# Expert stage of a two-layer backbone: two or five weight units converted late and none on GpSimd, plain group order in layer two, and in layer one each slot's row of g2 gathered from a table

## The chip, the cores and the metric

The kernel runs on one core of a Trainium2 chip. The metric is the device time of one execution in microseconds; the time shown is a median of runs, and one further execution was recorded by the profiler.

## The reference

Two layers run over a stream of 256 context tokens and 1024 latent tokens of width 1024. Each layer mixes tokens and then sends every token to two of 16 experts (top group of four, top two experts inside it). What matters here is the expert part:

```python
def expert_block(args):
    xblk, e = args
    return (jax.nn.silu(xblk @ w1[e]) * (xblk @ w3[e])) @ w2[e]
...
out = jnp.zeros((n_tok + 1, d), h.dtype).at[slot_tok].add(yb * slot_w[:, None])
...
        if last:
            x = x + g2 * hier_moe(h2, *moe_args).reshape(bsz, n_lat, d)
        else:
            ...
            f = hier_moe(jnp.concatenate([h2c, h2], axis=0), *moe_args)
            ctx = ctx + cg2 * f[:bsz * n_ctx].reshape(bsz, n_ctx, d)
            x = x + g2 * f[bsz * n_ctx:].reshape(bsz, n_lat, d)
```

So a token's expert output is scaled by its routing weight and by a row of 1024 gains. In layer one (`last` false) that row is `g2` for latent tokens and `cg2` for context tokens; in layer two only latent tokens are left and there is one row.

## The kernel before

**Blocks.** A router sorts tokens into slots by expert. An expert's slots are worked off in blocks of 128 rows; the expert stage walks the 16 experts in the order of the list `eo`, and for each of them runs first what goes beyond 128 slots (under `tc.If(cnt > P)`): a full second block (`block(x1, ...)`) if there are more than 192, and a half block of 64 rows (`block_half`) for what is left over or for 129 to 192 slots. Then comes the base block, `block(x0, ...)`, which every expert has. An expert with a base block alone is called small here. A block is two passes over the weight units 0 to 3 and 4 to 7 (w1 and w3, into `hps`), a product `g` (ScalarE L1654, VectorE L1655), its transpose on TensorE (L1637, `gtp`), and a pass over units 8 to 11 (w2, into `yps`).

**Weight units.** Each expert has 12 units of 128x1024 fp32 (512 KB). SyncE fetches them into eight buffers `eraw`. A unit is converted before use: ScalarE writes the rounded high part (L1578), then VectorE, or GpSimd for units 5 and 11, writes the rest (L1580). `mm3` multiplies high by high, high by low and low by high. Conversions of the next expert's units stand inside the base block of the expert before: `side(u)` is called after each step u = 0 to 11 and converts one unit or two. A converted unit goes to one of 13 buffers `ew`, so at most one unit more than an expert's own twelve fits.

**Slots.** `gather` (GpSimd indirect DMA, L1590) brings the token rows of a block from `h2s`; for the base and second block of the expert after next it is issued in `side`, for the third block at L1876. `prep` turns them around on TensorE (L1608, `xtp`) and splits them (L63, L64, L1611) inside the base block before. `scatter` multiplies by gain and weight (VectorE L1626 in layer one, L1624 in layer two) and adds the rows into `xb` by an indirect DMA (L1627).

**Gains.** In layer one the gain rows are built per block in `gain`: ScalarE scales one row (L1618), VectorE adds the other (L1619), with a weight that is zero for the tokens of the other kind. In layer two the row is the same for all slots.

**Order.** The engines work off their queues in the written order (`tc.manual_schedule()`). GpSimd's queue holds, for each base block: the scatter of the block before, the third block's gather, unit 5, two gathers, then the scatter, then unit 11. The indirect DMAs use eight semaphores in turn. Where a branch is skipped, GpSimd executes instructions (`ISA` in the listings) that bring these semaphores to the counts of the other path, and these wait until the transfers that still hold one have landed.

**What runs.** By the trace, the blocks of the 16 positions of `eo` are (F a second block, h a half block, B the base block): layer one, order of groups 0, 2, 1, 3: B, FhB, B, FhB, B, FhB, B, hB, B, FB, hB, FhB, B, FhB, B, B. Layer two, the same order of groups: FB, hB, B, B, FhB, hB, B, B, hB, hB, B, B, FhB, hB, B, B. There groups 1 and 3 hold the small experts.

## Time and profile before

| what | us |
|---|---|
| median of 3 runs | 2846.44 (2843.09 to 2849.04) |
| the profiled execution | 2843.8 |
| its span, first to last instruction | 2842.0 |
| mean granted TensorE clock in it | 0.946 of full speed |

The page of that execution gives PE 2531.7 us busy (89% of the span), DVE 1827.6 (64%), ACT 1244.5 (44%) and POOL 775.1 (27%). A share says little by itself: the program has stages with different limits. The two expert stages are the stretches from 932.3 to 1493.6 us and from 2277.5 to 2809.9 us of the span. A timeline row reads: start, length, engine, line, operation, output and input by the program's names, count, and in brackets how long the engine had been idle and what ended that. A row of the view by stretches has its length, then busy time and count of PE, PEld, DVE, ACT and POOL, the granted clock, the busy share of the DMA engines and GB/s.

### The profile page before, as it was taken

The page shows a single profiled execution, that of the slowest core. Times are in us where ns is not written, and L with a number is a line of the kernel's source. Part 1 is how long each engine was busy: PE and PEld are TensorE (multiplying, and loading weights), DVE is VectorE, ACT ScalarE, POOL GpSimd, SP SyncE. Part 2 cuts the span into 40 slices and gives each one's busy share as a digit, 9 for nine tenths or more (in the row PEclk, how much of TensorE's full clock was granted, in tenths as well). Part 3 has the DMA queues.
Part 4 walks back from the last instruction along what each step waited for, and adds up shares of the span by engine and source line. Part 5 has one row for each costly group of instructions (what it writes and reads, how often), then busy time and mean ns, then how long its engine had stood idle before and what let it go on. Part 6 is the DMA issues. An engine that isn't in the chain of part 4 may idle for free. (4 is left out here: it accounts for less than half of the span.)

```text
span 2842.0 us, 41623 instructions
## 1 busy us (share of the span) xinstructions
PE 2531.7 (89%) x15412; PEld 2127.4 (75%) x15412; DVE 1827.6 (64%) x3173; ACT 1244.5 (44%) x2060; POOL 775.1 (27%) x514
## 2 busy tenths in 40 slices
PE   6999998898898899899997999979989788989894
PEld 3878887788686677677776898868977666767673
DVE  3314665777478777776775317748866858587776
ACT  3313213566323555555554322127652346465453
POOL 0000113401144344344430001123023425354442
PEclk8999999999999899999998999999999889999997
DMA  8374217431224777787775352264223468596856
GB/s 297 114 241 140 83 69 204 86 73 31 98 112 158 251 249 250 242 274 225 242 236 185 99 173 79 75 163 87 66 63 110 171 238 306 186 322 211 312 187 245
DMA packets 159551, 493.68 MB, mean 174 GB/s; under 512 B 18896, under 2 KB 40016, under 8 KB 158768
## 3 DMA queue, kind: packets, MB, share of 16 engines
q1 hardware_dynamic: 110336, 361.14, 38.1%
q0 software_dynamic: 29312, 99.39, 12.0%
q10 hardware_dynamic: 19552, 28.84, 2.8%
q8 instruction: 176, 2.88, 0.4%
q14 instruction: 175, 1.43, 0.2%
HBM read 408.75 MB, written 79.15 MB: 172 GB/s over the span
## 5 line engine op out<-in xcount | busy, mean ns | idle before, releaser
L1580 DVE TENSOR_TENSOR ew<-eraw,ew 128x1024 fp32r<-128x1024 f32 x318 | 466.3, 1489 | 40.2 <-ACT ew L1578 35.3
L1578 ACT ACTIVATE ew<-eraw 128x1024 fp32r<-128x1024 f32 x384 | 390.9, 1054 | 73.7 <-DMA eraw<-in_experts_dram 61.2
L212 PE MATMUL ps<-hh,w 128*128 128x256 f32 x2096 | 289.4, 292 | 17.7 <-PEq L751 5.1
L1627 POOL DMA_INDIRECT xb<-yt,yx x54 | 182.1, 3372 | 431.6 <-DVE yt L1626 259.6
L212 PEld LDWEIGHTS ps<-hh,w 128*128 128x128 f32 x2096 | 269.2, 197 | 27.4 <-ACT hh L319 5.7
L67 PE MATMUL hps<-ew,x 128*128 128x512 f32 x656 | 275.8, 420 | 7.3 <-PEq L1831 3.6
L69 PE MATMUL hps<-ew,x 128*128 128x512 f32 x656 | 264.7, 403 | 3.2 <-DVE x L64 3.2
L962 DVE TENSOR_REDUCE mx<-S 128x1 f32<-128x1280 f32 (+1 forms) x144 | 196.9, 1370 | 107.9 <-PE S L957 106.4
L68 PE MATMUL hps<-ew,x 128*128 128x512 f32 x656 | 265.4, 405 | 0.0
L970 ACT ACTIVATE pe<-S,mx 128x1280 f32<-128x1280 f32 (+1 forms) x144 | 177.4, 1232 | 47.6 <-DVE mx L962 40.1
L1580 POOL TENSOR_TENSOR ew<-eraw,ew 128x1024 fp32r<-128x1024 f32 x66 | 178.4, 2703 | 17.2 <-ACT ew L1578 9.1
L956 PE MATMUL S<-kk,qh 128*128 128x512 f32 (+1 forms) x400 | 158.3, 396 | 17.5 <-ACT pe L970 8.6
L67 PEld LDWEIGHTS hps<-ew,x 128*128 128x128 f32 x656 | 129.4, 197 | 40.5 <-issue 9.5
L69 PEld LDWEIGHTS hps<-ew,x 128*128 128x128 f32 x656 | 128.3, 196 | 34.0 <-DVE x L64 3.6
L212 PE MATMUL ps<-hl,w 128*128 128x256 f32 x1048 | 149.4, 286 | 0.0
L68 PEld LDWEIGHTS hps<-ew,x 128*128 128x128 f32 x656 | 129.5, 197 | 25.6
L67 PE MATMUL ps<-wv,hh 128*128 128x256 f32 (+1 forms) x480 | 142.2, 296 | 0.0
L957 PE MATMUL S<-kk,ql 128*128 128x512 f32 (+1 forms) x400 | 140.8, 366 | 0.2 <-DMA ql<-qs 0.2
L212 PEld LDWEIGHTS ps<-hl,w 128*128 128x128 f32 x1048 | 138.0, 196 | 0.0
L69 PE MATMUL ps<-wv,hl 128*128 128x256 f32 (+1 forms) x480 | 138.0, 287 | 0.0
L1608 PE MATMUL xtp<-cs,xg 128*128 128x128 f32 x584 | 98.0, 297 | 44.7 <-DMA xg<-h2s,ix 37.8
L68 PE MATMUL ps<-wv,hh 128*128 128x256 f32 (+1 forms) x480 | 137.8, 287 | 0.0
(597 smaller groups left out, 5773.0 us busy)
## 6 DMA issues: line engine op xcount, KB each, us to landing
eraw<-in_experts_dram SPq DMA_DIRECT2D x384, 512.0 KB
s<-in_w_mod_dram SPq DMA_DIRECT2D x91, 512.0 KB
raw<-in_w_in_t_dram SPq DMA_DIRECT2D x28, 512.0 KB
xb<-xt POOLq DMA_DIRECT2D x18, 512.0 KB, 2.9
h2s<-tm POOLq DMA_DIRECT2D x18, 512.0 KB
kk<-ks SPq DMA_DIRECT2D x14, 640.0 KB
ks<-shl ACTq DMA_DIRECT2D x16, 512.0 KB
qs<-shl ACTq DMA_DIRECT2D x16, 512.0 KB
```

The lines of the kernel that those rows point to most:

```text
L67: nc.tensor.matmul(o, lhsT=lh, rhs=rh, start=start, stop=False)
L68: nc.tensor.matmul(o, lhsT=lh, rhs=rl, start=False, stop=False)
L69: nc.tensor.matmul(o, lhsT=ll, rhs=rh, start=False, stop=stop)
L212: nc.tensor.matmul(ps[:, o:o + 256], lhsT=wt[:, w_, k, :], rhs=h_[ci][:, k, :], start=w_ == 0 and h_ is hh and k == 0, stop=h_ is hl and k ...
L956: nc.tensor.matmul(S[:, j, :n], lhsT=qh[:, m, q1], rhs=kk[:, m, k0:k0 + n], start=True, stop=False)
L957: nc.tensor.matmul(S[:, j, :n], lhsT=ql[:, m, q1], rhs=kk[:, m, k0:k0 + n], start=False, stop=True)
L962: nc.vector.tensor_reduce(out=u["mx", m], in_=u["S", m], axis=AX.X, op=OP.max, negate=True)
L970: nc.scalar.activation(out=pe[:, :nk], in_=u["S", m], func=AF.Exp, bias=u["mx", m], scale=1.0, accum_out=acc)
L1578: nc.scalar.activation(out=w[:, 0, :], in_=raw, func=AF.Copy)
L1580: eng.tensor_tensor(out=w[:, 1, :], in0=raw, in1=w[:, 0, :].bitcast(F32), op=OP.subtract)
L1608: nc.tensor.transpose(tp[:, i, :], g[:, (4 * j + i) * P:(4 * j + i + 1) * P], ident)
L1627: nc.gpsimd.indirect_dma_start(out=xb, out_offset=bass.IndirectOffsetOnAxis(ap=yidx[0:n], axis=0), in_=yt[0:n], in_offset=None, compute_op ...
```

## The change

Five things are altered, all in the expert stage.

- The second half of every conversion is on VectorE; only the two of the first seven units at the start of a layer (units 3 and 6) stay on GpSimd.
- Of each expert's twelve units the last two or five are converted late: not in the base block of the expert before, but at the start of the expert's own work. `late` says how many: five for experts at even positions of `eo` in layer two and at odd ones in layer one, two for the rest, none for the first. `late_units` reserves their buffers and writes out the code three times, one for each path: five steps inside a second block (one after each step 0 to 4), all of them ahead of a half block that has no second block before it, or, in a new `Else`, ahead of the base block. `when` lists the steps of the base block at which the remaining seven or ten are converted.
- The eight `eraw` buffers are tiles of their own, so that a late unit's buffer can be refilled on each path.
- In layer two the groups are walked in the order 0, 1, 2, 3. With the blocks above that gives FB, B, hB, B, FhB, B, hB, B, hB, B, hB, B, FhB, B, hB, B.
- In layer one `gain` is an indirect DMA on GpSimd: for each slot it gathers row 0 or 1 of the table `rows2` in HBM (g2 and cg2) by the index `kx` (1 for a context token) into `yt`. It is issued at the start of the block. `scatter` then multiplies by the weight and by that row in one instruction, as in layer two, but with `yt` in place of the shared row. L1618 and L1619 are gone.

```diff
-            eo = [EPG * g + i for i in range(EPG) for g in (0, 2, 1, 3)]
+                kx = mp1.tile([P, NB * NE], I32, name="kx")
+                rows2 = dram.tile([2, D], F32, name=f"rows2{l}")
+                nc.scalar.dma_start(out=rows2, in_=modd[l, :, 5 * D:6 * D])
+            eo = [EPG * g + i for i in range(EPG) for g in ((0, 1, 2, 3) if last else (0, 2, 1, 3))]
+            late = [0] + [5 if (ei % 2 == 0) == last else 2 for ei in range(1, NE)]
...
-                nc.scalar.activation(out=w[:, 0, :], in_=raw, func=AF.Copy)
-                eng = eng or (nc.gpsimd if u in (5, 11) else nc.vector)
-                eng.tensor_tensor(out=w[:, 1, :], in0=raw, in1=w[:, 0, :].bitcast(F32), op=OP.subtract)
+                split(w[:, 0, :], w[:, 1, :], raw, eng)
+                free.append(raw)
...
+            def late_units(n):
+                todo = []
+                for _ in range(n):
+                    raw, w, nxt_ = raws.pop(0), wk.tile([P, 2, D], F32R, name="ew", tag="ew", bufs=13), None
+                    if seq:
+                        nxt_ = (raw, *seq.pop(0))
+                        raws.append(raw)
+                    todo.append((raw, w, nxt_))
+
+                def f(j):
+                    if j < n:
+                        raw, w, nxt_ = todo[j]
+                        split(w[:, 0, :], w[:, 1, :], raw)
+                        if nxt_:
+                            nc.sync.dma_start(out=nxt_[0], in_=experts[l, nxt_[1], nxt_[2]])
+                return [w for _, w, _ in todo], f
...
-            def gain(n, w, wc):
+            def gain(n, wc):
                 yt = wk.tile([P, D], F32, name="yt", tag="yt", bufs=YT)
                 if not last:
-                    nc.scalar.activation(out=yt[0:n], in_=g2b[1][0:n], func=AF.Copy, scale=wc[0:n])
-                    nc.vector.scalar_tensor_tensor(out=yt[0:n], in0=g2b[0][0:n], scalar=w[0:n], in1=yt[0:n], op0=OP.mult, op1=OP.add)
+                    nc.gpsimd.indirect_dma_start(out=yt[0:n], out_offset=None, in_=rows2,
+                                                 in_offset=bass.IndirectOffsetOnAxis(ap=wc[0:n], axis=0))
...
-                if last:
-                    nc.vector.scalar_tensor_tensor(out=yt[0:n], in0=y[0:n], scalar=w[0:n], in1=g2b[0][0:n], op0=OP.mult, op1=OP.mult)
-                else:
-                    nc.vector.tensor_tensor(out=yt[0:n], in0=y[0:n], in1=yt[0:n], op=OP.mult)
+                nc.vector.scalar_tensor_tensor(out=yt[0:n], in0=y[0:n], scalar=w[0:n], in1=(g2b[0] if last else yt)[0:n],
+                                               op0=OP.mult, op1=OP.mult)
...
                 gs = []
+                yt = gain(P, wc_)
                 for hf in range(2):
...
+                ws, finish = late_units(late[ei])
+                units = units + ws
...
                         def side1(u):
+                            finish(u)
...
                     with big.Else():
-                        block_half(x1, units, sw[:, col(e, 1)], swc[:, col(e, 1)], yx[:, col(e, 1)])
+                        for j in range(late[ei]):
+                            finish(j)
+                        block_half(x1, units, sw[:, col(e, 1)], None if last else kx[:, col(e, 1)], yx[:, col(e, 1)])
+                if late[ei]:
+                    with any_.Else():
+                        for j in range(late[ei]):
+                            finish(j)
...
+                when = [] if ei + 1 == NE else [0, 1, 2, 4, 6, 8, 10] if late[ei + 1] == 5 else [0, 1, 2, 3, 4, 6, 7, 8, 10, 11]
...
-                    for _ in range((0, 1, 1, 1, 1, 1, 1, 1, 1, 1, 1, 2)[u] if ei == 0 else (1, 1, 1, 1, 1, 1, 0, 1, 1, 1, 1, 2)[u]):
-                        nxt.append(load_unit(len(nxt)))
+                    if u in when:
+                        nxt.append(load_unit())
```

VectorE, layer one, the start of the base block of a small expert (position 2). Before, up to the product `g` of the first pass; the two rows at the head close the branch that this expert skips, and L1580 converts units of the next expert:

```order
L1832 UNCONDITIONAL_BRANCH
L1831 UNCONDITIONAL_BRANCH
L1580 TENSOR_TENSOR ew<-eraw,ew 128x1024
L1879 TENSOR_LOAD cnt_i
L1580 TENSOR_TENSOR ew<-eraw,ew 128x1024 x2
L1655 TENSOR_TENSOR g<-g,hps 128x256
```

The same place after the change (conversions stand under the helper's line L64, the product at L1676):

```order
L1851 UNCONDITIONAL_BRANCH
L64 TENSOR_TENSOR ew<-eraw_11530,ew 128x1024
L64 TENSOR_TENSOR ew<-eraw_11531,ew 128x1024
L1850 UNCONDITIONAL_BRANCH
L64 TENSOR_TENSOR ew<-eraw_11532,ew 128x1024
L1905 TENSOR_LOAD cnt_i
L64 TENSOR_TENSOR ew<-eraw_11533,ew 128x1024
L64 TENSOR_TENSOR ew<-eraw_11534,ew 128x1024
L1676 TENSOR_TENSOR g<-g,hps 128x256
```

Two conversions of the expert's own late units now stand ahead of the three of the next expert's.

GpSimd, layer one, a base block. Before, from the end of the skipped branch (`xg_11524` is the third block's rows, the row with 1408x1024 the scatter, L1580 units 5 and 11):

```order
L1831 UNCONDITIONAL_BRANCH
L1879 TENSOR_LOAD cnt_i
L1876 DMA xg_11524<-h2s,ix 128x1024
L1580 TENSOR_TENSOR ew<-eraw,ew 128x1024
L1738 COMPARE_AND_BRANCH
L1738 UNCONDITIONAL_BRANCH x2
L1590 DMA xg<-h2s,ix 128x1024 x2
L1627 DMA xb<-yt,yx 1408x1024
L1580 TENSOR_TENSOR ew<-eraw,ew 128x1024
```

After, the same stretch, with the instructions of the skipped branch at its head:

```order
L1850 ISA
L1850 UNCONDITIONAL_BRANCH
L1640 DMA yt<-rows_11526,kx 128x1024
L1905 TENSOR_LOAD cnt_i
L1902 DMA xg_11524<-h2s,ix 128x1024
L1757 COMPARE_AND_BRANCH
L1757 UNCONDITIONAL_BRANCH x2
L1612 DMA xg<-h2s,ix 128x1024 x2
L1647 DMA xb<-yt,yx 1408x1024
```

The gather of the gain rows stands first in the block, behind the skipped branch's `ISA`, and both conversions are gone.

VectorE, layer two, an expert whose first work is a half block. Before, after the branch the half block's own sums begin at once:

```order
L1624 SCALAR_TENSOR_TENSOR yt<-s,sw,g_34270 64x1024
L1862 UNCONDITIONAL_BRANCH x2
L1709 TENSOR_TENSOR s<-hps,s 64x512
L1711 TENSOR_TENSOR g<-g,s 64x256
L1709 TENSOR_TENSOR s<-hps,s 64x256
```

After, in a position with five late units:

```order
L1881 UNCONDITIONAL_BRANCH x2
L64 TENSOR_TENSOR ew<-eraw_34292,ew 128x1024
L64 TENSOR_TENSOR ew<-eraw_34285,ew 128x1024
L64 TENSOR_TENSOR ew<-eraw_34286,ew 128x1024
L64 TENSOR_TENSOR ew<-eraw_34287,ew 128x1024
L64 TENSOR_TENSOR ew<-eraw_34288,ew 128x1024
L1729 TENSOR_TENSOR s<-hps,s 64x512
```

Five conversions stand ahead of the half block's first sum.

## Rows read from the trace of the kernel before

**Rows 1.** Busy time by stretches: the expert stage of layer one, then of two.

```profile
932.30:1493.60 561.30, 520.34 (x2436) 412.12 (x2436) 409.82 (x492) 308.21 (x451) 222.51 (x105) 0.96 0.74 244
2277.53:2809.90 532.37, 475.34 (x2184) 371.23 (x2184) 373.22 (x437) 276.61 (x411) 226.18 (x104) 0.94 0.74 249
```

**Rows 2.** Waits of PE in layer one's expert stage: us in total, times, longest.

```profile
PE gtp L1637 <- DVE g L1655: 28.1, 6, 4.7
```

**Rows 3.** Waits of PE in layer two's expert stage, same columns.

```profile
PE xtp L1608 <- DMA xg<-h2s,ix: 27.0, 5, 6.7
PE gtp L1637 <- DVE g L1655: 10.2, 3, 3.4
...
PE hps L1686 <- DVE ew L1580: 4.1, 1, 4.1
```

**Rows 4.** By stretches, layer one: half block, base block, small expert's base block.

```profile
977.13:989.80 12.67, 12.67 (x69) 9.34 (x69) 5.26 (x13) 4.76 (x11) 1.59 (x1) 1.00 0.28 44
989.80:1009.43 19.63, 19.15 (x93) 15.29 (x92) 17.68 (x20) 15.40 (x22) 13.33 (x5) 1.00 0.65 212
1009.43:1035.13 25.70, 20.84 (x92) 16.78 (x93) 22.61 (x24) 15.89 (x21) 10.05 (x6) 0.93 1.02 360
```

**Rows 5.** By stretches, layer one: a usual second block, and the first one.

```profile
1035.13:1053.05 17.92, 17.91 (x86) 14.59 (x84) 9.44 (x14) 5.42 (x9) 4.76 (x2) 1.00 0.69 211
954.02:977.13 23.11, 19.91 (x85) 15.69 (x84) 13.76 (x17) 7.29 (x11) 10.26 (x5) 0.93 0.82 282
```

**Rows 6.** Timeline in that small expert's base block, which begins at 1009.43.

```profile
1013.02 1.21 DVE L1626 TENSOR_TENSOR yt<-yps,yt 128x1024 f32<-128x1024 f32 x1
1014.51 2.34 POOL L1627 DMA_INDIRECT xb<-yt,yx  x1 [5.92 <-DVE yt L1626]
...
1015.57 4.78 DVE L1580 TENSOR_TENSOR ew<-eraw,ew 128x1024 fp32r<-128x1024 f32 x1 [0.21 <-ACT g L1654]
...
1016.30 2.96 POOL L1580 TENSOR_TENSOR ew<-eraw,ew 128x1024 fp32r<-128x1024 f32 x1
...
1023.01 0.44 PE L1637 MATMUL gtp<-cs,g 128*128 128x128 f32 x2 [4.70 <-DVE g L1655]
...
1025.47 0.98 POOL L1876 DMA_INDIRECT xg<-h2s,ix  x1 [6.20 <-PE xtp L1608]
```

**Rows 7.** The conversions' second half, all: ns min/median/max, first and last start.

```profile
L1580 DVE TENSOR_TENSOR ew<-eraw,ew x318: 1206/1214/4816, 918.3 to 2796.5; 128x1024 fp32r<-128x1024 f32 x159
...
L1580 POOL TENSOR_TENSOR ew<-eraw,ew x66: 2370/2772/3319, 921.5 to 2798.7; 128x1024 fp32r<-128x1024 f32 x66
```

**Rows 8.** Timeline, layer one, half block from 1053.05, then base block from 1065.72.

```profile
1054.31 1.57 POOL L1627 DMA_INDIRECT xb<-yt,yx  x1 [9.98 <-DVE yt L1626]
...
1068.88 1.22 DVE L1626 TENSOR_TENSOR yt<-s,yt 64x1024 f32<-64x1024 f32 x1
...
1070.38 7.02 POOL L1627 DMA_INDIRECT xb<-yt,yx  x1 [14.49 <-DVE yt L1626]
```

**Rows 9.** The gathers of L1590, whole execution: us from issue to landing.

```profile
DMA to landing us min/median/max: 4.8/8.1/9.5
```

**Rows 10.** GB/s from 745 to 750 us in 40 slices: one row of `modd` to 128 partitions.

```profile
GB/s 0 0 0 0 0 0 0 0 0 0 0 197 197 229 426 360 360 393 360 393 426 164 262 197 131 33 33 33 0 0 0 0 0 0 0 0 0 0 0 0
```

**Rows 11.** Timeline, layer two: base block of position 1 from 2341.28, position 2's from 2360.57.

```profile
2345.79 7.04 POOL L1627 DMA_INDIRECT xb<-yt,yx  x1 [14.63 <-DVE yt L1624]
...
2359.58 1.33 POOL L1876 DMA_INDIRECT xg<-h2s,ix  x1 [6.75 <-ACT ew L1578]
...
2373.68 1.09 PE L1608 MATMUL xtp<-cs,xg 128*128 128x128 f32 x4 [5.87 <-DMA xg<-h2s,ix]
```

**Rows 12.** By stretches, layer two: the sum of the four pairs of small experts' blocks.

```profile
sum 205.02, PE 167.31 PEld 131.00 DVE 161.92 ACT 110.65 POOL 104.10; mean PE 41.83 PEld 32.75 DVE 40.48 ACT 27.66 POOL 26.03
```

**Rows 13.** By stretches, layer two: the stage's last base block.

```profile
2792.41:2809.90 17.49, 17.47 (x76) 13.76 (x76) 7.02 (x10) 3.79 (x8) 5.73 (x3) 1.00 0.44 108
```

**Rows 14.** By stretches, layer two: the sum of five half blocks that follow a base block.

```profile
sum 81.09, PE 71.50 PEld 52.24 DVE 46.46 ACT 19.55 POOL 33.43; mean PE 14.30 PEld 10.45 DVE 9.29 ACT 3.91 POOL 6.69
```

More of the change, by code (lines that the diff above doesn't have):

```diff
@@ L1596, in backbone_kernel @@
                 gg[b] = gather(ix[:, eo[0] + b * NE:eo[0] + b * NE + 1], f"xg{b}")
-            units = [load_unit(u, False, nc.gpsimd if u in (3, 6) else nc.vector) for u in range(7)]
+            units = [load_unit(False, nc.gpsimd if u in (3, 6) else nc.vector) for u in range(7)]
             for _ in range(7):
@@ L1668, in block @@
                             gtr(gs[1], 1)
-                        if (f, n) == (2, 0):
-                            yt = gain(P, wl_, wc_)
                         if (f, n) == (0, 1):
@@ L1682, in block_half @@
                 s = wk.tile([P, D], F32, name="s", tag="yt", bufs=YT)
+                yt = gain(R, wc_)
                 gs = []
@@ L1720, in block_half @@
                             gtr(*gs[2])
-                yt = gain(R, wl_, wc_)
                 for n in range(2):
@@ L1748, in backbone_kernel @@
                 pf(1, ("hpse", "hpse")[b])
-            units += [load_unit(u) for u in range(7, NUNIT)]
+            units += [load_unit() for u in range(7, NUNIT)]
             for c in g2b:
@@ L1838, in backbone_kernel @@
                         aim(f"third{l}_{ei}", cnt > 2 * P + P // 2)
-                        block(x1, units, sw[:, col(e, 1)], swc[:, col(e, 1)], yx[:, col(e, 1)], side1, "e")
+                        block(x1, units, sw[:, col(e, 1)], None if last else kx[:, col(e, 1)], yx[:, col(e, 1)], side1, "e")
                         with tc.If(cnt > 2 * P + P // 2, label=f"third{l}_{ei}") as big2:
-                            block(x2, units, sw[:, col(e, 2)], swc[:, col(e, 2)], yx[:, col(e, 2)], idle, "e")
+                            block(x2, units, sw[:, col(e, 2)], None if last else kx[:, col(e, 2)], yx[:, col(e, 2)], idle, "e")
                             with tc.If(cnt > 3 * P):
@@ L1892, in backbone_kernel @@
                     break
-                block(x0, units, sw[:, col(e, 0)], swc[:, col(e, 0)], yx[:, col(e, 0)], side, "")
+                block(x0, units, sw[:, col(e, 0)], None if last else kx[:, col(e, 0)], yx[:, col(e, 0)], side, "")
                 if ei + 1 < NE:
```

29 lines of the change are left out of this document (14 added, 15 removed).

## The prediction

> **What bounds the kernel now.** I read the busy time by stretches first. The two expert stages take 561.3 and 532.4 us, PE is busy for 520 and 475 of them, and the granted clock is 0.96 and 0.94 [rows 1]. PE sets the pace and loses time where it waits. So the second view is what PE waits for. In layer one it is six waits of up to 4.7 us for the product `g` on VectorE [rows 2]; in layer two five waits of up to 6.7 us for gathered rows, three for `g`, and one of 4.1 for a converted unit [rows 3]. The third view, block by block, gives the price of a wait. A base block that runs undisturbed takes 19.6 us at full clock; a small expert's takes 25.7 at a mean clock of 0.93 [rows 4]. Of the 6.1 us between them 4.7 are the wait, and 1.4 are matmuls after it at the lower of the clock's two levels (1.2 instead of 2.4 GHz). I keep 1.4 us as the price of the clock behind every wait of over 2 us.
>
> The timeline says why PE waits for `g` [rows 6]. A conversion on VectorE takes 1.21 us in the middle, but 4.8 at worst [rows 7]. The long one, from 1015.57, is joined after 0.7 us by a conversion on GpSimd that lasts until 1019.26, and ends 1.1 us behind it: the two exclude each other. While GpSimd only issues the scatter (from 1014.51) nothing is lengthened. Four conversions stand between the block's last instruction on VectorE and the next `g`, one of them 3.6 us too long, and PE stands still for 4.70.
>
> **Layer one, what goes.** With no conversion on GpSimd the lock goes. It cost six small experts' blocks (positions 2, 4, 6, 8, 12, 14) their wait; position 1's second block took 23.1 us instead of 17.9 [rows 5] for the same reason, and I count these 5 us as a full gain. The 62 conversions that move to VectorE take 62 x 1.21 = 75 us there in the whole execution; the lock took about as much, and L1618 and L1619 leave too, so VectorE's load doesn't grow. What matters is what stands ahead of each `g`.
>
> **Layer one, what comes in.** Ahead of a small expert's `g` now stand the scatter's multiplication, one conversion, two late ones and three of the next expert, six where there were four. The multiplication also waits for the gathered gains. The half block's scatter before it holds GpSimd for 7.02 us, from 1070.38, 4.7 us into the base block [rows 8]. So the gain gather is issued some 12 us into that block, takes 1 to 2 us, and lands 8.1 us later [rows 9], 21.7 us after the block's start, or 2.1 into the small expert's block. From there: 1.3 for the multiplication and six times 1.2 end at 10.6, `g` at 11.0. PE asks for it 8.9 us into the block (1023.01 less 4.70, less 1009.43) [rows 6]. The wait is then 2.1 us instead of 4.7: 6 x 2.6 = **15.6 us** saved, the clock's part not. Ends: no wait (28 and the clock's 8), or a wait as long as before (0).
>
> The gather itself has no row. Its rows in HBM are two, read over and over. The nearest is the broadcast of one row of `modd` to 128 partitions: it moved 512 KB within 2.1 us (17 slices) at up to 426 GB/s [rows 10], so a repeated row costs nothing by itself, and I take the token gathers' 8.1 us under load; the ends are 4.8 and 9.5 [rows 9]. Their bytes are no bound: 29 gathers of at most 512 KB are 15 MB over 561 us, 27 GB/s beside the 244 that flow [rows 1].
>
> A half block needs a gather of 64 rows. A scatter of 128 rows holds GpSimd for 1.57 us, one of 64 rows for 7.02 [rows 8]. I take the long time for the gather of 64 rows as well. Behind the second block's scatter (1055.9) it is issued by 1063.2 and lands, with the DMA engines nearly idle then (share 0.28 in [rows 4]), after 4.8 to 8.1 us: 1068.0 to 1071.3, where VectorE wants it at 1068.9. Queued behind that wait are the three conversions and the `g` of the base block that follows. Five such places, 0 to 4 us each: I take **+3 us** for all, ends 0 and 20.
>
> Position 7 (a half block first) has five late conversions ahead of its own sums: +3. The last position gets five ahead of its base block and a late last gather, which holds up the scatter that the next layer waits for: +3 (0 to 6). Layer one: -15.6 - 5 + 3 + 3 + 3 = **-12 us**, between -40 and +20.
>
> **Layer two.** There the gathers of token rows are late. Behind a half block GpSimd issues a scatter for 7.04 us and then waits 6.75 more, by the listing in a skipped branch or for a semaphore, until it has landed; only 18.3 us into the base block the three gathers start [rows 11]. A conversion of at least 2.4 us [rows 7] stands between them, and PE waits 5.87 us in the next block, which is a small expert's; a second small one follows directly, and both are starved, since three base blocks in a row want 36 units. The four pairs of small blocks take 205.0 us [rows 12].
>
> The new order puts a larger expert before every small one. The landing stays, the conversion on GpSimd goes: the gather arrives 2.4 us sooner, and with fewer units fetched in that time perhaps another us. I take a wait of 2.5 us, ends 0 and 5. The wait for `g` is then covered: without a gain gather the multiplication starts about 1 us into the block instead of 2.1, and `g` is done at 9.9. Six small blocks take 19.6 + 2.5 + 1.4 = 23.5; position 1's, whose expert before has no half block, 19.6 + 1.1 = 20.7; the last block 17.5 as now [rows 13]. Together 179.2 instead of 205.0: **-25.8**.
>
> The stage's first two blocks lose one wait for rows (4.2 of the 27.0 us) since GpSimd's third conversion no longer stands ahead of the gathers, and half of the 4.1 us for a unit [rows 3]: with the clock -7.6. Five half blocks that come first in their expert take 81.1 us, 16.2 each against 12.7 undisturbed [rows 14, 4]. They had one conversion and a lock of about 3 us ahead of their sums and get five conversions, 6.1 us: up to 1.9 more each, I take +4 for all (0 to +10). Layer two: -25.8 - 7.6 + 4 = **-29 us**, between -60 and -10.
>
> **Sum.** -12 - 29 = -41. Against the profiled execution's own 2843.8 that is 2802.8; its span is 1.8 less and moves with it. The median is 2.6 above that execution, so the forecast is **2805 us**.
>
> On the landing the trace and a rule can be weighed. The rows give 4.8 to 9.5 us for 512 KB [rows 9]. The Trainium skill, "DMA: Bandwidth & Descriptors", section "Anatomy of one DMA — SWDGE (gpsimd) path", fits 2.0 us plus the bytes at 436 GB/s, which is 3.2 us as an estimate for 512 KB. By that the gain gather would never be late, the small blocks of layer one would wait 1.1 us instead of 2.1, and the sum would be -47. No gather here lands that fast, so the sum goes by the rows.
>
> **Rivals.**
> - The gains come late: the 64-row gathers land at the slow end and stop VectorE in five half blocks (+17 more), and the small blocks wait as long as before (+15.6). Layer one ends at +20, layer two at -25: about -5 to -20, **2833**. For it: three conversions and a `g` that PE needs stand right behind the wait. Against it: the DMA engines are nearly idle when the 64-row gather runs. 0.17.
> - Both waits vanish: with less to fetch, gathers land in 5 to 6 us; small blocks are at 20 in both layers, half blocks at 13 to 14. -62 to -85, **2773**. For it: a lone broadcast moved in 2.1 us. Against it: the DMA share is 1.02 and 360 GB/s in a small block [rows 4]. 0.15.
> - Slower. A gain gather is held by more than its landing: in a small expert's block it can't be issued before the scatter of the block before has landed, 11 us after that scatter's start (1014.51 to 1025.47 [rows 6]). It then lands about one us after that block's end. Each us more on a landing costs PE about two per pair of experts, one in each base block, with seven pairs 14 us. Layer two's 29 us and layer one's 12 are used up at a landing 3 us longer than taken, 11 us. At 12 us it is 2805 + 14 x 3.9 = **2860**, at 15 us 2900. For it: all 128 descriptors read one row of HBM while the experts' units stream. The Trainium skill, "SBUF — State Buffer", section "SBUF: two separate sides", adds that descriptors for a GpSimd DMA can't be written while VectorE holds the shared port pair in some of its modes; more conversions on VectorE would then stretch the issue. Against it: the broadcast [rows 10], and a scatter that was issued beside conversions in 2.34 us instead of 1.57 [rows 6, 8]. 0.08.
> - The order doesn't do what it says: layer two's small blocks stay at 26 to 28 because the gathers wait for the same landing. Layer two gives -8, the sum is about -20 to 0, **2835**. 0.05.
>
> **How the numbers follow.** The forecast (-22 to -62, 2784 to 2824) has 0.55. A difference of 0.2%, 5.7 us, is about what runs of this kernel can tell from none. Faster by more: all of the forecast and of the second rival, most of the first (0.13) and of the last (0.03), 0.86. Slower by more: the third, and a rest of the first, 0.08. Within it: 0.06. The range runs from the far end of the second rival to the near part of the first and last: 2764 to 2837, leaving out some 0.18.
>
> **What would show it.** No GpSimd conversion beyond the first seven units, and no VectorE conversion over 1.3 us behind them, show the lock gone. In layer one, `gtp` waits of about 2 us in the six small blocks and multiplications that wait for a gather of `yt` show the working above; waits of 4 or more show the first rival, a landing of `yt` over 11 us the third. In layer two, `xtp` waits of 2 to 3 us in six blocks, and small blocks at 23 to 24 us; half blocks first in their expert near 17. If the 64-row gather holds GpSimd for 1 us, layer one gains more than said. The forecast is wrong if VectorE's queue has a wait that I haven't placed: each us ahead of a `g` is paid by PE.

## The result and the profile after

The changed kernel takes **2781.66 us** (median of 4 runs, 2775.79 to 2783.96) against 2844.77 for the kernel before in the same rounds: a ratio of **0.9775, 95% interval 0.9753 to 0.9798**, 63 us less. The profiled execution took 2781.0 us, with a span of 2779.2. In the sections below, differences of medians are worked out from such ratios, times 2844.8 us, since each group of runs had its own runs of the kernel before. One of e5's four executions took 4840.5 us, a slow run that its ratio leaves out.

Both expert stages by stretches (columns as in [rows 1]):

```profile
935.07:1471.80 536.73, 515.51 (x2436) 403.08 (x2436) 373.19 (x496) 284.45 (x426) 151.10 (x104) 0.98 0.80 276
2265.08:2750.95 485.87, 460.03 (x2186) 358.57 (x2184) 358.61 (x477) 277.47 (x414) 116.47 (x72) 0.98 0.81 276
```

Layer one is 24.6 us shorter than in [rows 1], layer two 46.5. What lies outside the stages is 8.3 us longer: the first stage begins 2.8 us later, 9.3 more lie between the stages, and 3.8 less behind the second. What PE waited for, layer one first:

```profile
PE gtp L1657 <- DVE g L1676: 10.9, 8, 3.9
PE hps L67 <- PEq L1850: 5.4, 2, 4.3
PE hps L1706 <- DVE s L1729: 4.3, 1, 4.3
...
PE hps L1706 <- DVE s L1729: 11.6, 5, 2.5
PE gtp L1657 <- DVE g L1676: 6.9, 7, 1.0
PE hps L67 <- PEq L1850: 3.0, 1, 3.0
```

The six long waits of [rows 2] and all waits for gathered rows of [rows 3] are gone. New are a wait for `g` of 1.0 us in the larger experts' base blocks (14 in both layers), the 3.9 in the stage's very first block, and waits of 1.6 to 4.3 us for the sums of half blocks that come first. Block by block, the stretches that answer to [rows 4] (half block, base block, small expert's base block):

```profile
980.33:993.41 13.08, 12.79 (x68) 9.37 (x69) 5.21 (x12) 3.73 (x10) 2.53 (x2) 1.00 0.34 63
993.41:1014.25 20.84, 19.69 (x93) 15.21 (x92) 17.13 (x22) 14.64 (x21) 7.78 (x5) 1.00 0.70 231
1014.25:1033.71 19.46, 19.29 (x92) 15.54 (x93) 17.06 (x22) 12.98 (x19) 6.14 (x5) 1.00 1.03 384
```

The small block fell from 25.7 to 19.5 us: with the wait the clock's part is back too (1.00 for 0.93). The base block ahead of it rose from 19.6 to 20.8. VectorE in that small block (timeline):

```profile
1014.55 1.27 DVE L1645 SCALAR_TENSOR_TENSOR yt<-yps,sw,yt 128x1024 f32<-128x1024 f32 x1
1015.74 6.89 DVE L64 TENSOR_TENSOR ew<-eraw,ew 128x1024 fp32r<-128x1024 f32 x6
1022.56 0.41 DVE L1676 TENSOR_TENSOR g<-g,hps 128x256 f32<-128x256 f32 x1
```

The multiplication starts 0.3 us into the block, the gain rows are there, six conversions stand ahead of `g`, and `g` ends 8.7 us in; PE asks for it at 8.9. The conversions of layer one behind the first units, all of them (ns min/median/max), lie within 20 ns, where [rows 7] had 4816 as the worst:

```profile
L64 DVE TENSOR_TENSOR ew<-eraw,ew x175: 1209/1217/1228, 958.6 to 1460.6; 128x1024 fp32r<-128x1024 f32 x175
```

The gain gathers hold GpSimd for 0.9 to 1.9 us, those of 64 rows for 0.9 to 1.3, and this is their landing (us from issue, min, median, max; the trace has it for four of the 29):

```profile
L1640 POOL DMA_INDIRECT yt<-rows,kx x29: 920/975/1926, 950.7 to 1465.2; - x29
...
DMA to landing us min/median/max: 6.1/9.3/10.5
```

And the scatter behind a half block, which held GpSimd for 7.02 to 7.06 us before [rows 8, 11], took 3.3. In layer two (GpSimd, timeline; the base block starts at 2343.45):

```profile
2347.95 3.29 POOL L1647 DMA_INDIRECT xb<-yt,yx  x1 [15.15 <-DVE yt L1645]
2357.19 1.91 POOL L1902 DMA_INDIRECT xg<-h2s,ix  x1 [5.95 <-DMA xb<-yt,yx]
2359.40 1.41 POOL L1612 DMA_INDIRECT xg<-h2s,ix  x1 [0.30 <-PE gtp L1657]
```

The gathers begin 13.7 us into the block; in [rows 11] it was 18.3.

### The profile page after: what moved, and what is told of

Same layout as the page of the kernel before. It is cut to its first block, busy times and chain, and to the rows that moved or that the text cites. A ratio compares the mean times of both kernels' runs of the same rounds, so it can differ in the third digit from the quotient of the medians.

```text
span 2779.2 us, 41446 instructions
## 1 busy us (share of the span) xinstructions
PE 2515.4 (91%) x15412; PEld 2102.6 (76%) x15412; DVE 1768.2 (64%) x3204; ACT 1215.0 (44%) x2031; POOL 590.6 (21%) x481
## 3 DMA queue, kind: packets, MB, share of 16 engines
q0 software_dynamic: 33040, 112.76, 13.3%
## 5 line engine op out<-in xcount | busy, mean ns | idle before, releaser
L64 DVE TENSOR_TENSOR ew<-eraw,ew 128x1024 fp32r<-128x1024 f32 x380 | 454.1, 1229 | 66.9 <-ACT ew L63 56.9
L212 PE MATMUL ps<-hh,w 128*128 128x256 f32 x2096 | 288.6, 292 | 19.0 <-ACT hh L319 5.3
L212 PEld LDWEIGHTS ps<-hh,w 128*128 128x128 f32 x2096 | 268.8, 197 | 28.3 <-ACT hh L319 6.3
L67 PE MATMUL hps<-ew,x 128*128 128x512 f32 x656 | 269.2, 410 | 13.1 <-PEq L1850 8.4
L68 PE MATMUL hps<-ew,x 128*128 128x512 f32 x656 | 261.4, 398 | 0.0
L69 PE MATMUL hps<-ew,x 128*128 128x512 f32 x656 | 261.3, 398 | 0.0
L1647 POOL DMA_INDIRECT xb<-yt,yx x54 | 132.2, 2448 | 442.6 <-DVE yt L1645 442.6
L67 PEld LDWEIGHTS hps<-ew,x 128*128 128x128 f32 x656 | 124.8, 190 | 46.4 <-issue 14.8
L212 PE MATMUL ps<-hl,w 128*128 128x256 f32 x1048 | 149.1, 286 | 0.0
L69 PEld LDWEIGHTS hps<-ew,x 128*128 128x128 f32 x656 | 124.5, 190 | 30.6 <-DVE x L64 0.4
L68 PEld LDWEIGHTS hps<-ew,x 128*128 128x128 f32 x656 | 125.0, 191 | 26.1
L212 PEld LDWEIGHTS ps<-hl,w 128*128 128x128 f32 x1048 | 137.5, 195 | 0.0
L990 PE MATMUL atp<-cs,pe 128*128 128x128 f32 x656 | 109.5, 282 | 30.3 <-DVE pe L978 23.8
L67 PE MATMUL yps<-ew,ghl 128*128 128x512 f32 x328 | 136.7, 417 | 0.0
```

Of the source, the lines that this page charges most:

```text
L64: (eng or nc.vector).tensor_tensor(out=lo, in0=src, in1=hi.bitcast(F32), op=OP.subtract)
L67: nc.tensor.matmul(o, lhsT=lh, rhs=rh, start=start, stop=False)
L68: nc.tensor.matmul(o, lhsT=lh, rhs=rl, start=False, stop=False)
L69: nc.tensor.matmul(o, lhsT=ll, rhs=rh, start=False, stop=stop)
L212: nc.tensor.matmul(ps[:, o:o + 256], lhsT=wt[:, w_, k, :], rhs=h_[ci][:, k, :], start=w_ == 0 and h_ is hh and k == 0, stop=h_ is hl and k ...
L990: nc.tensor.transpose(tp[:, j * P:(j + 1) * P], u["pe0"][:, (j0 + j) * P:(j0 + j + 1) * P], ident)
```

## The experiments

My theory: the lock between conversions on GpSimd and on VectorE (the two exclude each other) had cost nearly all that was gained, and the other parts bring little or cost. The main rival: late units are what frees VectorE. Each kernel was timed beside the kernel before:

| run | median us | ratio, 95% interval | layer one | layer two |
|---|---|---|---|---|
| before | 2844.77 | 1 | 561.3 | 532.4 |
| after | 2781.66 | 0.9775 (0.9753-0.9798) | 536.7 | 485.9 |
| e1 before, no GpSimd conversion | 2744.42 | 0.9649 (0.9627-0.9672) | 520.7 | 473.6 |
| e2 before, plain order | 2837.75 | 0.9977 (0.9963-0.9991) | 557.6 | 523.4 |
| e3 after, old gain | 2777.57 | 0.9773 (0.9747-0.9800) | 536.4 | 483.6 |
| e4 after, one GpSimd conversion | 2798.28 | 0.9831 (0.9802-0.9859) | 536.1 | 499.2 |
| e5 after, none late | 2759.86 | 0.9693 (0.9664-0.9723) | 534.9 | 467.4 |
| e6 after, buffers in turn | 2774.64 | 0.9761 (0.9728-0.9793) | 532.6 | 487.5 |
| e7 e1 and plain order | 2742.94 | 0.9635 (0.9607-0.9664) | 520.6 | 468.9 |
| e8 after, late units spread in half blocks | 2788.30 | 0.9787 (0.9761-0.9813) | 537.1 | 495.2 |
| e9 e7, half block scatters 128 rows | 2770.39 | 0.9729 (0.9713-0.9745) | 530.1 | 488.6 |
| e10 e7 and the gather | 2747.40 | 0.9656 (0.9640-0.9672) | 523.3 | 474.4 |
| e11 e7, even conversions | 2750.22 | 0.9667 (0.9651-0.9683) | 522.8 | 470.8 |
| e12 e7 with a hole | 2732.91 | 0.9596 (0.9572-0.9620) | 521.3 | 463.0 |

The last two columns are the stages of each profiled execution, cut at the same instructions.

**e1: no conversion on GpSimd, nothing else altered.**

```diff
-                eng = eng or (nc.gpsimd if u in (5, 11) else nc.vector)
+                eng = eng or nc.vector
```

> The kernel before with units 5 and 11 converted on VectorE; nothing else. Theory (the lock between a GpSimd and a VectorE conversion makes the small blocks of layer one late): no VectorE conversion over 1.3 us behind the first seven units, the gtp waits of layer one fall from 28.1 us to under 8, small blocks from 25.7 to 20-21, and gathers of layer two start 2.4 us earlier; 2805 to 2822 us in all. Rival (spreading the conversions by late units is what frees VectorE, the lock is a side issue): the waits for g stay over 20 us, 2838 to 2850. On the scatter of 64 rows that held GpSimd for 7.0 us before and 3.3 after: if an unbroken run of VectorE conversions beside it stretches it, it stays at 6.5 to 7.1 here; if GpSimd's own conversions made it long, it falls to 3.5 or less.

It gained 100 us, more than the whole change and more than I expected of it. PE's waits in layer one and the group of ScalarE's conversions on the page (busy, mean ns, idle before and its cause), both e1, then what SyncE's fetches waited for in the kernel before:

```profile
PE gtp L1637 <- DVE g L1655: 9.2, 7, 1.9
...
L1578 ACT ACTIVATE ew<-eraw 128x1024 fp32r<-128x1024 f32 x384 | 389.2, 1054 | 18.4 <-DMA eraw<-in_experts_dram 9.8
...
SPq L1572 <- POOL ew L1580: 260.4, 58, 11.8
```

The waits for `g` fell from 28.1 to 9.2 us, and ScalarE waited 9.8 us for fetched units, where the kernel before waited 61.2 (53.8 of it in layer two). The second number I had not looked at: a conversion that takes 2.4 to 3.3 us on GpSimd, behind that engine's gathers, also gives its fetch buffer back late. SyncE waited for that 58 times in the kernel before, 260 us in all; in e1 twice, 4 us. The lock itself is seen in more than the one place of [rows 6]: in the kernel before, all 38 VectorE conversions over 1.3 us overlap one on GpSimd, and 36 of them end 1.1 us behind it. So the edit takes away three things at once, the lock, the late buffers and the conversion that stood between GpSimd's gathers; what each is worth it does not show. The rival falls. The scatter behind half blocks stayed at 7.0 us, so it isn't GpSimd's conversions that stretch it.

**e4: a part of the lock put back.** One conversion of each expert goes to GpSimd again, in the changed kernel.

```diff
-                split(w[:, 0, :], w[:, 1, :], raw, eng)
+                split(w[:, 0, :], w[:, 1, :], raw, eng or (nc.gpsimd if u == 5 else None))
...
-                        nxt.append(load_unit())
+                        nxt.append(load_unit(u=len(nxt)))
```

> The changed kernel with one conversion of each expert (the sixth of the next expert's units) back on GpSimd. Theory (lock): GpSimd's conversion takes 2.4 to 3.3 us and stretches one or two VectorE conversions by 1 to 3.6 us each; where it falls ahead of a product g or of the scatter's gathers PE waits; 2790 to 2805 us, with VectorE conversions of 2.4 us and more in the trace. Rival (one conversion less on VectorE pays for the lock): 2775 to 2785.

16 us slower than the changed kernel, with 13.3 us more in layer two of the profiled execution; VectorE's longest conversion is 4.0 us. As the theory says.

**e2 and e7: the order, with and without the lock.**

```diff
-            eo = [EPG * g + i for i in range(EPG) for g in (0, 2, 1, 3)]
+            eo = [EPG * g + i for i in range(EPG) for g in ((0, 1, 2, 3) if last else (0, 2, 1, 3))]
```

> The kernel before with the groups of layer two walked 0, 1, 2, 3; nothing else. Theory (two small blocks in a row starve the conversions and the gathers): the waits for gathered rows in layer two fall from 27.0 us to 10-15, small blocks from 26.8 on average to 23-25, 2822 to 2835 us. Rival (the gathers wait for the same landing of the half block's scatter, whatever the order): small blocks stay at 26 to 28, 2840 to 2850.

> The kernel before with units 5 and 11 on VectorE and the plain order in layer two. Theory (the order pays once the lock is gone, since the five waits for rows of 2 to 3 us that are left are in the first of two small blocks): small blocks of layer two 20 to 21 us, no wait over 1 us, 2726 to 2736 us. Rival (the order is worth nothing, the scatter of 64 rows still holds GpSimd for 7 us ahead of the gathers): 2740 to 2748, with waits of 2 to 3 us in six small blocks.

Alone it is worth 0.2%; without the lock 4 us against e1, which the intervals don't separate. In both the rival was nearer: four or five small blocks of layer two still wait for rows behind the half block's scatter (4.1 to 5.8 us in four of them in e2; 7.8 us in five waits in e7, 2.8 at most, and one of 1.8 put down to VectorE).

**e3 and e10: the gather.** e3 builds the gains in the changed kernel as before; e10 puts the gather into e7.

```diff
-                    nc.gpsimd.indirect_dma_start(out=yt[0:n], out_offset=None, in_=rows2,
-                                                 in_offset=bass.IndirectOffsetOnAxis(ap=wc[0:n], axis=0))
+                    nc.scalar.activation(out=yt[0:n], in_=g2b[1][0:n], func=AF.Copy, scale=wc[0:n])
+                    nc.vector.scalar_tensor_tensor(out=yt[0:n], in0=g2b[0][0:n], scalar=w[0:n], in1=yt[0:n], op0=OP.mult, op1=OP.add)
...
```

(The cut shows e3; e10 makes the opposite edit in e7.)

> The changed kernel with the gain rows built on ScalarE and VectorE as before, in place of the gather. Theory (the gather takes 1.28 us of VectorE and about 1 of ScalarE off each of 29 blocks, and the path from VectorE's queue to g is just full): waits for g grow by 1 to 2 us in the small blocks, 2787 to 2800 us. Rival A (VectorE has room, the gather brings nothing): 2779 to 2785. Rival B (the gathers' landings cost more than they save, as in the half block of position 7): 2768 to 2778.

> The kernel without GpSimd conversions and with the plain order (the seventh experiment), and the gain rows gathered from the table as in the changed kernel; the eight fetch buffers rotate as before, none is late. It differs from the fifth experiment in the place of the fetch buffers alone. Theory (the fetch buffers as tiles of their own lie on memory of the stage before, their first fetch waits 33 us for it, and the first base block is short of units): the first base block of layer one falls from 28.3 to 23-24 us, layer one from 534.9 to 521-529, 2741 to 2752 us. Rival (the gather's own issue and landing cost the 14 us): layer one 532 to 537, 2755 to 2762.

On the whole time neither shows a gain: no difference in e3, and e10 is 6 us slower than e7 (the intervals overlap; 5.6 us of it lie in layer two, which has no gain gather). But e3's zero is a sum. Its first block takes 21.3 us where the changed kernel's takes 27.1, for a reason that isn't the gather (see e5). Its six small blocks of layer one take 127.8 us where the changed kernel's take 117.1, and five of them have the wait for `g` that the theory expected, 1.1 to 2.0 us. So beside late units the gather saves some 11 us in these blocks; without them it saves nothing there (126.9 us in e10, 125.9 in e7).

**e5: no late units.**

```diff
-            late = [0] + [5 if (ei % 2 == 0) == last else 2 for ei in range(1, NE)]
+            late = [0] * NE
```

(with `when` listing twelve steps.)

> The changed kernel with no late units: all twelve of the next expert's units are converted in the base block before, on VectorE; the gather and the plain order stay. Theory (the lock is the whole gain, and what the late units bring costs: five conversions ahead of a half block, and a buffer that comes free two or three steps later): larger experts' base blocks 19.1 to 19.6 us without a wait for g, half blocks first in their expert near 13, 2733 to 2750 us. Rival (the gather or the order is what costs): 2765 to 2785. The scatter of 64 rows: 6.5 to 7.1 us if VectorE's unbroken run beside it is what stretches it, 3.3 if the gather or the order shortened it.

23 us faster than the changed kernel; the late units cost. Larger base blocks are at 19.3 and the half blocks that come first at 12.9 in layer two. Not all of it was loss: the small blocks take 128.9 and 162.9 us in the two layers of e5, 117.1 and 156.8 with late units. It stays 10 us behind e10 (the intervals just touch). There the fetch buffers `eraw` rotate as before, here they are tiles of their own; in a stage's first block e5 also has a conversion at step 0 that e10 has at step 6, which my expectation of e10 overlooked. SyncE's longest wait for fetching ahead of the first stage, in e5:

```profile
SPq L1578 <- POOL tm L1439: 33.2, 1, 33.2
```

and the first base block of layer one, e5, e10, then e3:

```profile
932.37:960.69 28.32, 23.89 (x93) 18.76 (x93) 21.41 (x26) 21.00 (x26) 9.39 (x7) 0.81 1.03 408
...
931.49:952.91 21.42, 21.42 (x92) 17.31 (x93) 18.80 (x23) 18.65 (x24) 5.71 (x5) 0.88 1.01 396
...
932.20:953.49 21.29, 21.29 (x93) 17.29 (x93) 15.89 (x22) 15.01 (x20) 2.84 (x3) 0.88 1.02 394
```

The first fetch waits 33.2 us until GpSimd is through with `tm` of the stage before (I take it that the tiles lie on its memory), and starts 23 us ahead of the stage, in e10 54. The first block is short of units: 6.9 us. e3 says that it is the wait and not the conversion at step 0: it has that conversion and tiles of its own, but two more tiles stand ahead of them, its fetch doesn't wait for `tm` and starts 30 us ahead of the stage, and its first block takes 21.3 us. The changed kernel has the same wait as e5, and one of 24.7 us ahead of layer two.

**e6: buffers in turn.** In the changed kernel the third unit of the next expert gets the buffer of unit 3 or 4, not of unit 1: the allocator gives out buffers in the order in which it holds them to be free, and with late units that is no longer the order of use.

```diff
+            ew_t = [wk.tile([P, 2, D], F32R, name=f"ew{i}", tag=f"ew{i}", bufs=1) for i in range(13)]
+            def ring():
+                ew_t.append(ew_t.pop(0))
+                return ew_t[-1]
...
-                w = wk.tile([P, 2, D], F32R, name="ew", tag="ew", bufs=13)
+                w = ring()
```

> The changed kernel with the 13 buffers for converted units handed out in strict turn. In the changed kernel the third unit of the next expert gets the buffer of unit 3 or 4, which PE gives back two or three steps later, and g stands behind that conversion. Theory (this is the wait of 1.0 us in 13 base blocks of larger experts): these go from 20.8 to 19.6, and the half blocks' waits stay; 2762 to 2772 us. Rival A (three conversions in a row stretch the scatter of 64 rows to 5 to 7 us again, the gathers behind it come late and the waits for rows of 2 to 3 us return in the small blocks of layer two): 2776 to 2795. Rival B (another wait takes its place at once): 2778 to 2784 with base blocks at 20.8.

Both parts came true at once. The wait on PE, here in the changed kernel (ScalarE, timeline), is gone, and larger base blocks take 19.3 us instead of 20.8:

```profile
2350.64 1.06 ACT L63 ACTIVATE ew<-eraw 128x1024 fp32r<-128x1024 f32 x1 [3.10 <-PE hps L69]
```

But the scatter behind a half block is back at 7.0 us (GpSimd, e6), and with it four waits for rows of 1.8 to 3.2:

```profile
2339.76 7.03 POOL L1652 DMA_INDIRECT xb<-yt,yx  x1 [16.65 <-DVE yt L1650]
2354.51 1.32 POOL L1907 DMA_INDIRECT xg<-h2s,ix  x1 [7.72 <-PEq L1855]
```

What is left is 0.1%, within the intervals. So the misplaced buffer cost 1.5 us in each of 14 base blocks, and gave most of it back through a hole in VectorE's conversions.

**e9 and e12: what the scatter waits for.** e9 asks whether 64 rows are the reason; e12 makes such a hole in e7.

```diff
-                                             in_=yt[0:n], in_offset=None, compute_op=OP.add)
+                                             in_=yt[0:m], in_offset=None, compute_op=OP.add)
...
+                nc.gpsimd.memset(yt[R:P], 0.0)
...
-                scatter(yt, s, R, wl_, yidx)
+                scatter(yt, s, R, wl_, yidx, P)
```

```diff
-                    for _ in range((0, 1, 1, 1, 1, 1, 1, 1, 1, 1, 1, 2)[u] if ei == 0 else (1, 1, 1, 1, 1, 1, 0, 1, 1, 1, 1, 2)[u]):
+                    for _ in range((0, 1, 1, 1, 1, 1, 1, 1, 1, 1, 1, 2)[u] if ei == 0 else (1, 1, 0, 0, 2, 1, 1, 1, 1, 1, 1, 2)[u] if last and ei % 2 == 0 else (1, 1, 1, 1, 1, 1, 0, 1, 1, 1, 1, 2)[u]):
```

> The kernel without GpSimd conversions and with the plain order (the seventh experiment), and in a half block the scatter writes all 128 rows, the upper 64 of them zeros (set by GpSimd ahead) for the rows that stand for no token. Theory (a scatter of 128 rows gets through a run of VectorE conversions in 2.3 us, one of 64 rows only behind the run): the scatter after a half block takes 1.6 to 3.5 us instead of 7.0, the gathers behind it start some 4 us earlier, and the four waits for rows of 1.8 to 2.9 us in layer two fall below 1: 2727 to 2737 us. Rival (the place decides, not the number of rows: the run of conversions behind a half block holds any scatter): 7.0 us stays, 2740 to 2748.

> The kernel without GpSimd conversions and with the plain order (the seventh experiment); in layer two, in the base blocks of the experts at even positions, the third and fourth conversion move from the third and fourth step to the fifth, where two stand. That leaves VectorE some 1.5 us without a conversion behind the second, as in the changed kernel. Theory (the scatter behind a half block ends 1.3 us after VectorE's run of conversions does): the scatter takes 3.3 us instead of 7.0, lands and frees GpSimd 4 to 5 us earlier, and the four waits for rows of 1.8 to 2.9 us in layer two's small blocks fall below 0.7; 2727 to 2737 us. Rival A (the scatter's 7 us are not the run's): 7.0 stays, waits stay, 2740 to 2748. Rival B (the scatter is short but the conversions pushed back make g late by as much): 3.3 us and 2738 to 2746.

GpSimd in e9, where the base block starts at 2324.96:

```profile
2329.97 6.69 POOL L1628 DMA_INDIRECT xb<-yt,yx  x1 [11.28 <-DVE yt L1625]
2345.67 1.01 POOL L1878 DMA_INDIRECT xg<-h2s,ix  x1 [9.01 <-DMA xb<-yt,yx]
```

128 rows in the same place are held for 6.7 us, so it is the place, not the rows; twice the bytes land later, the gathers start 20.7 us into the block, and the kernel is 27 us slower than e7. VectorE, then GpSimd in e7 at such a place:

```profile
2318.92 3.48 DVE L1580 TENSOR_TENSOR ew<-eraw,ew 128x1024 fp32r<-128x1024 f32 x3
2322.32 0.41 DVE L1655 TENSOR_TENSOR g<-g,hps 128x256 f32<-128x256 f32 x1
2322.65 2.35 DVE L1580 TENSOR_TENSOR ew<-eraw,ew 128x1024 fp32r<-128x1024 f32 x2
...
2319.27 7.02 POOL L1627 DMA_INDIRECT xb<-yt,yx  x1 [11.76 <-DVE yt L1624]
2333.55 1.02 POOL L1876 DMA_INDIRECT xg<-h2s,ix  x1 [7.26 <-DMA xb<-yt,yx]
```

and GpSimd at the same place in e12:

```profile
2316.86 3.28 POOL L1627 DMA_INDIRECT xb<-yt,yx  x1 [11.78 <-DVE yt L1624]
2326.89 1.43 POOL L1876 DMA_INDIRECT xg<-h2s,ix  x1 [6.75 <-PE gtp L1637]
```

In e7 five conversions run with 0.25 us between the third and the fourth, in which VectorE works at `g`, and end at 2325.00; the scatter ends at 2326.29. In e12 the third conversion begins 0.66 us behind the second, which ends at 2318.86 (VectorE works at `g` and then idles for 0.33), and the scatter ends at 2320.14. Each time that is 1.3 us behind the run. The gathers start 4.3 us earlier in their block, the waits for rows in layer two's small blocks are gone, and these take 19.7 to 20.2 us. The stage fell by 5.9 us, as the theory says; the ratios differ by 0.4% with intervals that still overlap, so the mechanism is shown by the blocks, and the size in the whole time is not settled. e12 is faster than both kernels: 4.0% under the kernel before, 51 us under the changed one.

**e8 and e11: two whose theory failed.** e8 spreads the late units over a half block's passes; e11 puts one conversion at each step in e7.

```diff
-                        for j in range(late[ei]):
+                        for j in range(2):
                             finish(j)
-                        block_half(x1, units, sw[:, col(e, 1)], None if last else kx[:, col(e, 1)], yx[:, col(e, 1)])
+                        block_half(x1, units, sw[:, col(e, 1)], None if last else kx[:, col(e, 1)], yx[:, col(e, 1)], finish)
...
+                    if side:
+                        side(2 + hf + q0)
```

```diff
-                    for _ in range((0, 1, 1, 1, 1, 1, 1, 1, 1, 1, 1, 2)[u] if ei == 0 else (1, 1, 1, 1, 1, 1, 0, 1, 1, 1, 1, 2)[u]):
+                    for _ in range((0, 1, 1, 1, 1, 1, 1, 1, 1, 1, 1, 2)[u] if ei == 0 else 1):
```

> The changed kernel with the late units of a half block that comes first in its expert spread over its passes: two ahead, one behind each pass's product. Theory (the five conversions ahead of its sums cost it a wait of 2.5 us, 4.3 in layer one): half blocks first in their expert fall from 15 to 18 us to 13 to 14.5, 2764 to 2774 us. Rival (VectorE is full there and the wait only moves to a later pass): 2776 to 2784.

> The kernel without GpSimd conversions and with the plain order (the seventh experiment), with one conversion at each of the twelve steps instead of none at the seventh and two at the last. Theory (one conversion less stands ahead of g in the next block): the six waits for g of 1.3 us in layer one's small blocks go, 2730 to 2738 us. Rival (VectorE has about 21 us of work in a small block and the wait only moves): 2739 to 2747.

Both came out slower than theory and rival said, e8 by 3 us against the changed kernel and e11 by 9 against e7, both within the intervals. In both the wait moved. In e8 the half blocks wait 3.0 us for the transposed product instead of 2.5 for the sums; in e11 the five waits of 1.3 us in layer one's small blocks became six of 0.9 to 1.2, and its larger base blocks got one of 1.0 each.

## Why the prediction was right or wrong

The sign and the mechanism of the lock were right. 41 us were forecast and 63 came: just past the 22 to 62 that the forecast gave itself, inside the full range. That the sum came so near is in part luck, since terms were off in both directions:

| step | forecast | measured |
|---|---|---|
| layer one, six small blocks | -15.6 | -37.2 |
| layer one, position 1's second block | -5 | -4.9 |
| layer one, half blocks behind a second block | +3 | +1 |
| layer one, position 7's half block | +3 | +4.2 |
| layer one, last position | +3 | +0.2 |
| layer one, larger experts' base blocks, position 0 and the rest | none | +17.6 |
| layer one, position 10's half block | none | -5.2 |
| layer two, first two blocks | -7.6 | -7.5 |
| layer two, eight small blocks | -25.8 | -48.2 |
| layer two, five half blocks first | +4 | -1.8 |
| layer two, larger experts' base blocks | none | +11 |
| outside the stages | none | +8.3 |

- **The small blocks of layer one.** Three steps of this term were off. The first is the scatter of 64 rows at 7.02 us, which I took for a property of 64 rows and gave to the gather as well. It is a property of the place: 3.3 us in the changed kernel, and the gathers of 64 rows took 0.9 to 1.3. I had named that last as a sign of a larger gain in layer one. So the gain gather is issued 8.1 us into the base block instead of 12; ahead of the small block shown above it landed 8.2 us later, 4.5 before the base block's end. The second is the landing: the 8.1 us of [rows 9] count from the issue (and come from five of the 64 gathers), and I added the 1 to 2 us that the issue takes. The third is the clock's 1.4 us a block, which I left out of the gain, for a wait of 2.1 us that didn't come. How much hangs on the scatter e6 shows, where it is back at 7.03 us (GpSimd and VectorE, timeline; the base block starts at 989.31, the small one at 1008.62):

```profile
1001.15 1.93 POOL L1645 DMA_INDIRECT yt<-rows,kx  x1 [0.30 <-DVE x L64]
...
1010.13 1.29 DVE L1650 SCALAR_TENSOR_TENSOR yt<-yps,sw,yt 128x1024 f32<-128x1024 f32 x1 [1.12 <-DMA yt<-rows,kx]
```

  The gather is issued 11.8 us into the base block, as I had it, and the multiplication waits for it as I had it, but it starts 1.5 us into the small block and PE waits 0.9 us for `g`, at full clock. The six blocks take 138.6 us by my sum, 122.8 in e6 and 117.1 in the changed kernel. So of the 21.6 us that this term was short, some 16 come without the shorter scatter (the other two steps make six times 1.4 and 1.2), and some 6 with it.
- **The small blocks of layer two.** The same step, in part: "the landing stays" was wrong, since the landing is counted from a scatter that holds GpSimd 3.7 us less. The wait of 2.5 us that I kept in six blocks is there in four of them in e6 (1.8 to 3.2 us) and in e7 (1.8 to 2.8). Of 179.2 us by my sum e6 leaves 164.4, the changed kernel 156.8. The larger part of the gain needs no new order at all: in e1 the same eight blocks take 170.3 us instead of 205.0. That e7 gains only 4 us on e1 shows that I gave the order too much of it.
- **Larger base blocks.** I asked in the last sentence for a wait in VectorE's queue that I hadn't placed; this is it. Three conversions stood ahead of `g` before and after, but the third now waits for a buffer that PE still reads; the order of the queues, which I had read, doesn't show it, and e6 does.
- **Outside the stages and position 0.** I had costed the fetch buffers as tiles of their own at nothing. e5 against e10 shows the price, 10 us; in the profiled executions it is 11.6 more in layer one and 5.5 between the stages, and 7.0 less in layer two, which stays unexplained. Position 0's block is 5.3 of the 17.6 in the table. From the end of layer one's stage to the next layer's first matmul of L212 the six kernels with such tiles (the changed one, e3 to e6, e8) take 34 to 37 us and the eight others 26 to 29.
- **Half blocks first.** Right in kind (five conversions ahead of the sums, waits of 1.6 to 4.3 us); I overstated the net, since what they lose with GpSimd's conversions was worth more: layer two's five take 63.7 us in e1, 81.1 before.
- **The rivals.** What the second one said of the waits is what happened, and the costs above took 9 us of its time away. A landing over 11 us, the third, is not among the four that the trace has. The fourth was wrong for the changed kernel, yet near to the truth in e2, where the scatter takes 7 us and six small blocks are at 25 to 29 us; in e7 the waits are there and shorter.
- **The rules weighed.** On the landing the rows decided rightly: of the four that the trace has none came near 3.2 us, the shortest took 6.1. The Trainium skill, "SBUF — State Buffer", section "SBUF: two separate sides", says that descriptors for a GpSimd DMA can't be written while VectorE holds the shared port pair in some of its modes; I left it to the slow rival. The conversions here read two operands from SBUF, and the traces agree in one place, behind half blocks, where scatters end 1.3 us behind VectorE's run of conversions (e7, e12). Behind full blocks they don't: there a scatter took 2.34 us beside a run of six. Behind half blocks it bears on a part of the terms that I had wrong.

Put in the order of the edits, by ratios: no conversion on GpSimd -100 us (e1), the plain order -4 (e7), the gather +6 (e10), fetch buffers of their own +10 (e5), late units +23 (the changed kernel). Of these the second and third lie within their intervals, and the third holds for this order only (e3).

## What to carry to other kernels

Before pricing a wait behind a shared resource, try the smallest edit that takes the sharing away: here one line gained more than the change that it was part of. A duration that is constant in a trace is not a property of the instruction; look at what runs beside it at each place before giving it to a neighbour. And when buffers are allotted out of turn, or moved to other memory, read which instruction frees them: out of turn cost 1.5 us here in each of 14 blocks, moving them about 10 us in all. A total that doesn't change can hide two changes (e3, e6); the blocks tell them apart.

## What was not expected of the hardware

- A scatter behind a half block ends 1.3 us (1.28 to 1.34) behind VectorE's run of conversions, whether the run has two (3.3 us), four (5.9, once in e6) or five (7.0 us); with 128 rows it is 1.44 to 1.48 (e9). The length of a pause doesn't tell where the run ends: 0.25 us between two conversions, filled by `g`, don't end it (e7); 0.66 with 0.33 of idle time do (e12), and so do 0.39 us of idle time behind position 10's half block in layer one of the changed kernel and 0.13 at the same place in e3. Behind a full block a scatter takes 2.34 us beside a run of six conversions, up to 3.5 in e1 and e7. What tells the two places apart stays open; it is neither the number of rows (e9) nor GpSimd's conversions (e1), the gather or the order (e5).
- The gathers that read two rows of HBM over and over landed after 6.1, 8.2, 10.4 and 10.5 us, in the four places that the trace has; five gathers of distinct token rows in the kernel before took 4.8 to 9.5. That is too few to say whether the repeated rows cost anything.
